# Two experts of up to 64 rows kept on chip in layer 0, slots spread over the partitions, and the modulation product cut along its contraction

## The chip, the cores and the metric

The kernel runs on one core of one Trainium2 chip. The metric is the device time of one execution in microseconds (us), taken as the median over several runs. PE is TensorE, which multiplies matrices, DVE is VectorE, ACT is ScalarE, POOL is GpSimd and SP is SyncE, which here only issues transfers. Weights, gathered rows and results move by DMA between device memory and the chip's buffer.

## The reference, cut to what matters

There are two layers over 512 latent and 256 context tokens of width 1024. Each layer has six modulation vectors, a trunk of four mixers, and a mixture of 32 experts; two experts of one group are chosen for each token.

```python
mod = c_act @ w_ada + b_ada                  # and the same for the context's c
sh1, sc1, g1, sh2, sc2, g2 = jnp.split(mod[:, None, :], N_MOD, axis=-1)
h = modulate(rms_norm(x, norm1_g), sh1, sc1)
...                                          # z = h @ w_in, four mixers, x = x + g1 * merge_groups(...)
h2 = modulate(rms_norm(x, norm2_g), sh2, sc2)
def expert_block(args):
    xb, e = args
    return (jax.nn.silu(xb @ w_gate[e]) * (xb @ w_up[e])) @ w_down[e]
y = y_buf[dest].reshape(n_tok, TOP_K_INNER, d).astype(jnp.float32) * gates[..., None]
x = x + g2 * jnp.sum(y, axis=1)              # layer 0: for 768 tokens, layer 1: for the 512 latent ones
```

All is f32. One expert has 6.29 MB of weights, so the 32 experts of a layer are 201 MB, which are read once in each layer.

## The kernel before, in words

The order on each engine is fixed when the program is built. A layer is a trunk (modulation, the projections `zunits`, the mixers) and then `moe(l)`.

**Modulation.** `w_ada` of a layer (1024 x 6144) is cut into 12 column blocks of 512, `ada(l, j)`, 24 in all; both layers' blocks are computed in trunk 0. The stationary operand is the activated conditioning, two rows (latent and context). A block's four 128-column pieces go to the four column quarters of the array, each through all eight chunks of the contraction: 32 matmuls of 128 columns (L267). Four DVE additions of 2 x 128 (L274) then put each quarter, with the bias, into its own piece of `mrow`. Where the vector is wanted per feature (shift and scale), four small transposes (L280) and a copy into `mcol` (L281) follow; the others go to device memory (`modd`, L293) and are read back, broadcast over the partitions, by `bc` (L301).

**Experts.** Experts are taken by rank of their row count. `CAP` gives the rows that each rank may have, and the number of 32-row steps in it (4 to 1) is its class. The order is ranks 0 and 1, whose weights are loaded ahead of routing; then an interleaving that keeps a running sum of `COST` (a cost by class) near its mean; and last the ranks that stay on chip. PE works through `seq`: gate and up product of place 0, then for each place e gate and up of e (`gu`) and the down product of e-1 (`d`). Weights are issued on SP in the order `lseq`, in half-megabyte slots: 8 for `gu`, 4 for `d`, 34 in layer 0. A load waits until the work that last used its slots is done with them. For each place the gathered rows are transposed (`xTw`), multiplied (L1414), passed through the activation on ACT (L1429) and DVE (L1430), transposed (`hT`) and multiplied by the down weights.

**The end of a layer.** The result of a place below the tail is scaled and scattered by POOL to `yd` (L1762). When the last of these scatters is issued, the layer reads `yd` back, two rows for each token: `yload` (L1804), 1 MB for each group of 128 tokens, six groups (`t`) in layer 0 and four in layer 1, on POOL, into weight slots. The reads stand in `lseq` between weight loads. `accumulate` then weights the two rows (L1491 on ACT, L1494 on DVE), multiplies by the gate `g2` in layer 0 (L1495) and adds to `xres` (L1496). `g2` is read back from `modd` when the last scatter is issued. The tail places (four ranks of up to 32 rows) are not scattered: `tail_rows` (L1482) scales the down result into 32 rows each of one 128-row tile, and a one-hot matrix G, scaled by `tail_scale` (L1366), returns them to their tokens by the matmuls `tailw` (L1791), whose result is added to `xres` (L1792). `finish` takes the sum of squares and its reciprocal root (`rx`, L1814), and the next trunk starts with the normalised and transposed rows (`diag`, L377; `ht`, L334), the `hi` and `lo` parts of its weights (L169, L175) and the products `zunits` (L194 to L196).

```python
for at, ts in ((("gu", NE - 2), range(0, T // 2)), (("d", NE - 3), range(T // 2, T))):
    i = lseq.index(at) + 1
    lseq[i:i] = [("y", t) for t in ts]
```

## Time and profile before

| | |
|---|---|
| median of 3 runs (lowest to highest) | 1895.16 us (1893.27 to 1897.12) |
| time of the profiled execution | 1894.95 us |
| its span, first to last instruction | 1893.2 us |
| trunk 0 and routing / experts of layer 0 | 0 to about 481 / about 481 to 1052 us |
| trunk 1 and routing / experts of layer 1 | to about 1361 / to 1893 us |
| PE busy, DVE busy in the span | 1730.5 us (91%), 744.1 us (39%) |

The stages are read from which lines run when. PE's busy share includes overlapping matmuls and half-speed stretches, so it is no measure of how near a stage is to its limit. The granted clock tells at which speed PE ran; DMA share is the mean busy share of the core's 16 DMA engines.

### The profile page before, as it was taken

What the parts mean: (1) busy time and instruction counts of PE and PEld (TensorE: products, weight loads), DVE (VectorE), ACT (ScalarE), POOL (GpSimd) and SP (SyncE); (2) the same over time, 40 slices, a digit from 0 to 9 for tenths busy, and PEclk for the clock granted to TensorE, in tenths of its full rate; (3) what the DMA queues carried; (4) which work ended last, traced back from release to release, by engine and by line L of the source; (5) the groups of instructions that cost most, each with busy time, mean ns of one, the idle gap of its engine ahead of it and who ended that gap; (6) DMA issues with size and microseconds to landing.
All of it is one profiled execution on the core that took longest, in us unless ns stands there. A gap on an engine that the chain in (4) does not pass through costs nothing.

```text
span 1893.2 us, 32583 instructions
## 1 busy us (share of the span) xinstructions
PE 1730.5 (91%) x12876; PEld 999.2 (53%) x12876; DVE 744.1 (39%) x1627; ACT 467.2 (25%) x842; POOL 221.7 (12%) x253
## 2 busy tenths in 40 slices
PE   6999999998899999999985999999699999989975
PEld 3788788876343433333331788776444433323331
DVE  3666466546211111111116666665523232221135
ACT  4453364322121111111111654732200000000001
POOL 1000100113111111100010001002311110000010
PEclk9999999999799999999986999999799999999987
DMA  8358965453899999999968423428399999999995
GB/s 305 107 188 275 318 227 184 160 211 141 339 414 407 399 398 396 398 401 411 387 229 319 147 87 106 140 76 303 129 366 411 414 410 411 404 401 404 409 414 226
DMA packets 169022, 561.90 MB, mean 297 GB/s; under 512 B 22562, under 2 KB 49250, under 8 KB 139808
## 3 DMA queue, kind: packets, MB, share of 16 engines
q1 hardware_dynamic: 141616, 499.68, 68.9%
q0 software_dynamic: 23072, 54.17, 7.8%
q10 hardware_dynamic: 4176, 5.91, 0.9%
q8 instruction: 104, 1.70, 0.4%
q14 instruction: 54, 0.44, 0.1%
HBM read 544.22 MB, written 35.52 MB: 306 GB/s over the span
## 4 chain that ended last, share of the span: by engine, by line
PE 25%; DMA 18%; DVE 3%; issue 3%; ACT 1%; POOL 0%; SPq 0%; POOLq 0%; ACTq 0%; DVEq 0%
DMA u<-in_w_down 6%; PE gate_up L1414 6%; PE down L1414 3%; DMA u<-in_w_gate 3%; PE zunits L194 2%; PE zunits L195 2%; PE zunits L196 2%; DMA u<-in_w_up 2%; DMA xb<-in_w_down 2%; DMA xb<-in_w_up 1%; DMA xa<-in_w_up 1%; PE transP L838 1%; DMA xc<-in_w_gate 1%; DMA xc<-in_w_up 1%; PE tailw L1791 1%
## 5 line engine op out<-in xcount | busy, mean ns | idle before, releaser
L1414 PE MATMUL gate_up<-u,XT 128*32 128x256 f32 (+4 forms) x1664 | 277.3, 489 | 12.3 <-DMA u<-in_w_up 9.2
L1429 ACT ACTIVATE eh<-gate_up 64x256 f32<-64x256 f32 (+4 forms) x87 | 43.7, 502 | 766.5 <-PE gate_up L1414 745.0
L1414 PE MATMUL gate_up<-xb,XT 128*32 128x256 f32 (+4 forms) x1152 | 215.0, 483 | 12.0 <-DMA xb<-in_w_up 10.6
L1414 PEld LDWEIGHTS gate_up<-u,XT 128*32 128x32 f32 (+4 forms) x1664 | 92.2, 123 | 149.3 <-issue 106.9
L1414 PE MATMUL gate_up<-xa,XT 128*32 128x256 f32 (+4 forms) x680 | 149.8, 488 | 5.3 <-DMA xa<-in_w_up 2.9
L1430 DVE TENSOR_TENSOR eh<-eh,gate_up 64x256 f32<-64x256 f32 (+4 forms) x87 | 50.4, 580 | 256.4 <-ACT eh L1429 253.6
L194 PE MATMUL zunits<-hT,hi 128*128 128x512 f32 (+1 forms) x384 | 140.2, 366 | 0.9 <-ACT cqs L688 0.8
L195 PE MATMUL zunits<-hT,hi 128*128 128x512 f32 (+1 forms) x384 | 136.4, 355 | 0.1
L196 PE MATMUL zunits<-hT,lo 128*128 128x512 f32 (+1 forms) x384 | 135.5, 353 | 0.0
L1414 PE MATMUL gate_up<-xc,XT 128*32 128x256 f32 (+4 forms) x440 | 123.6, 502 | 5.5 <-DMA xc<-in_w_up 4.9
L1414 PEld LDWEIGHTS gate_up<-xb,XT 128*32 128x32 f32 (+4 forms) x1152 | 69.1, 121 | 112.1 <-issue 80.1
L1383 DVE COPY XT<-xTw 128x256 f32<-128x256 f32 (+6 forms) x64 | 44.0, 689 | 209.1 <-PE gate_up L1414 201.8
L1414 PE MATMUL down<-u,ehT 128*32 128x256 f32 (+4 forms) x656 | 109.9, 505 | 5.7 <-DMA u<-in_w_down 5.6
L1762 POOL DMA_INDIRECT yd<-ey,dst x56 | 52.2, 933 | 492.6 <-DVE ey L1474 239.2
L1414 PE MATMUL down<-xb,ehT 128*32 128x256 f32 (+4 forms) x592 | 91.9, 490 | 5.6 <-DMA xb<-in_w_down 5.6
L1474 DVE TENSOR_TENSOR ey<-down,bc 32x256 f32<-32x256 f32 (+7 forms) x112 | 57.7, 515 | 97.1 <-PE down L1414 95.9
L1381 PEld LDWEIGHTS xTw<-cpack,xb 96*128 96x128 f32 (+6 forms) x512 | 61.7, 200 | 51.8 <-issue 22.8
L1381 PE MATMUL xTw<-cpack,xb 96*128 96x96 f32 (+6 forms) x512 | 72.1, 283 | 17.7 <-DVE XT L1383 7.0
L175 DVE TENSOR_TENSOR lo<-u,hi 128x1024 fp32r<-128x1024 f32 (+2 forms) x54 | 65.5, 1217 | 46.0 <-ACT hi L169 45.4
L1472 ACT COPY ey<-down 64x512 f32<-64x512 f32 (+6 forms) x102 | 50.5, 495 | 133.7 <-PE down L1414 132.9
L194 PEld LDWEIGHTS zunits<-hT,hi 128*128 128x128 f32 x384 | 72.8, 190 | 16.0 <-issue 4.4
L1451 DVE COPY ehT<-hT 128x256 f32<-128x256 f32 (+4 forms) x47 | 19.6, 418 | 154.2 <-PE hT L1449 153.7
(397 smaller groups left out, 2898.9 us busy)
## 6 DMA issues: line engine op xcount, KB each, us to landing
u<-in_w_gate SPq DMA_DIRECT2D x112, 512.0 KB
u<-in_w_up SPq DMA_DIRECT2D x106, 512.0 KB
u<-in_w_ada SPq DMA_DIRECT2D x96, 512.0 KB
u<-in_w_down SPq DMA_DIRECT2D x89, 512.0 KB
xb<-in_w_gate SPq DMA_DIRECT2D x37, 1024.0 KB
xb<-in_w_down SPq DMA_DIRECT2D x37, 1024.0 KB
xb<-in_w_up SPq DMA_DIRECT2D x35, 1024.0 KB
xa<-in_w_down SPq DMA_DIRECT2D x26, 1024.0 KB
```

What stands on the lines that cost most here:

```text
L175: self.nc.vector.tensor_sub(o, v, h.bitcast(F32))
L194: mm(out, a[0], b[0], start=start, stop=False)
L195: mm(out, a[0], b[1], start=False, stop=False)
L196: self.lastm = mm(out, a[1], b[0], start=False, stop=stop)
L1381: nc.tensor.transpose(ps[:, k * 128:k * 128 + W], Xv[:, :, k], self.ident[a:a + W, a:a + W])
L1383: nc.vector.tensor_copy(xt, ps.rearrange("p (k n) -> p k n", k=8)[:, :, 0:W])
L1414: self.lastm = self.nc.tensor.matmul(o, x[:, k, a:a + w], m[k // q][:, k % q, c], start=(k == 0), stop=(k == K - 1), tile_position=(0, b))
L1429: self.lasta = nc.scalar.activation(v, ps[0:r, 0:c], AF.Silu)
L1430: self.lastv = nc.vector.tensor_mul(v, v, ps[64:64 + r, 0:c])
L1472: self.nc.scalar.copy(y[a:a + w, c], p[0:w, :])
L1474: self.nc.vector.tensor_mul(y[a:a + w, c], p[0:w, :], g2[b:b + w, c])
L1762: nc.gpsimd.indirect_dma_start(out=self.yd[l][:, :], in_=y, in_offset=None, out_offset=bass.IndirectOffsetOnAxis(ap=R["dst"][0:cap[e], ord ...
```

## The change

The change has these parts.

- Each `CAP` is rounded up to a multiple of 32. The classes of the ranks, and with them the matmul streams, are the same numbers as before: four of class 4, nine of 3, fourteen of 2 and five of 1 in layer 0.
- `TAIL` keeps ranks 25 and 26 (up to 64 rows each) on chip in layer 0, in place of ranks 28 to 31 (up to 32 rows each). `COST` changes slightly. The class of each place in layer 0 was `33142242224224222224232323331111` (with ranks 28 to 31 last) and is `33114141414222232232232322323322`; layer 1 keeps its order.
- In layer 0 all six reads of `yd` now follow the last weights in `lseq`. `g2` is read three scatters earlier. Two groups are accumulated after `gu` of place 31, two after `d` of place 30, and two in the loop over `tailw`. In layer 1 the accumulations stand earlier: one after `gu` of place 30, three after `d` of place 29.
- A table `spread` replaces the plain count in the one-hot comparisons, so that neighbouring rows of an expert lie 4 partitions apart in each block of 32. Which row of an expert lies where is all that differs.
- `ada`: each column quarter takes two of the eight chunks of the contraction and all 512 columns, which makes 8 matmuls of 512 columns in place of 32 of 128; four DVE additions of 2 x 512, each on the sum of the one ahead, add the quarters.

```diff
-CAP = ((96,) * 2 + (128,) * 3 + (104, 96) + (80,) * 4 + (72,) * 2 + (64,) * 3 + (56,) * 5 + (48,) * 5 + (40,) + (32,) * 3
...
+CAP = ((96,) * 2 + (128,) * 4 + (96,) * 7 + (64,) * 14 + (32,) * 5,
+       (96,) * 2 + (96,) * 8 + (64,) * 10 + (32,) * 12)
...
-NTL = 4
+TAIL = ((25, 26), (28, 29, 30, 31))
...
-COST = (24, 19, 13, 8)
+COST = (23, 18, 12.5, 8)
...
-        for k in range(8):
+        for a in range(2):
             for i in range(4):
-                nc.tensor.matmul(ps[32 * i:32 * i + 2, 0:128], self.act[:, k, :],
-                                 w[k // 2][:, k % 2, i * 128:(i + 1) * 128], start=(k == 0), stop=(k == 7),
-                                 tile_position=(0, 32 * i))
+                k = 4 * a + i
+                nc.tensor.matmul(ps[32 * i:32 * i + 2, :], self.act[:, k, :], w[k // 2][:, k % 2, :], start=(a == 0),
+                                 stop=(a == 1), tile_position=(0, 32 * i))
...
         for i in range(4):
-            nc.vector.tensor_add(row[:, i * 128:(i + 1) * 128], ps[32 * i:32 * i + 2, 0:128],
-                                 br[:, i * 128:(i + 1) * 128])
+            nc.vector.tensor_add(row, ps[32 * i:32 * i + 2, :], row if i else br)
...
-        a = slice(32 * j, 32 * j + 32)
-        for n, p in enumerate(py):
-            c = slice(n * 256, (n + 1) * 256)
+        w = py[0].shape[0]
+        a, n = slice(w * j, w * j + w), D // len(py)
+        for i, p in enumerate(py):
+            c = slice(i * n, (i + 1) * n)
             self.lastv = self.nc.vector.tensor_mul(Yr[a, c], p, Gs[a, c])
...
+        self.spread = pp.tile([128, 128], F16, name=f"spread{l}")
+        sv = self.spread.rearrange("p (b c r) -> p b c r", b=4, c=8)
+        for b in range(4):
+            nc.scalar.copy(sv[:, b], self.iota[:, 32 * b:32 * b + 32].rearrange("p (r c) -> p c r", r=4))
...
-        for at, ts in ((("gu", NE - 2), range(0, T // 2)), (("d", NE - 3), range(T // 2, T))):
+        for at, ts in ((("d", NE - 1), range(T)),) if l == 0 else ((("gu", NE - 2), (0, 1)), (("d", NE - 3), (2, 3))):
...
-        na = dict(zip((("gu", NE - 2), ("d", NE - 3), ("gu", NE - 1), ("d", NE - 2)), (1, T // 3, T // 3, 1)))
+        na = {("gu", NE - 1): 2, ("d", NE - 2): 2} if l == 0 else {("gu", NE - 2): 1, ("d", NE - 3): 3}
...
+                    if j == -4 and l == 0:
+                        g2 = [self.bc(self.buf(True), l, 3, m) for m in range(2)]
                     if j == -1:
                         written.append(True)
-                        if l == 0:
-                            g2 = [self.bc(self.buf(True), l, 3, m) for m in range(2)]
...
+        late = list(acc)
         for t in range(T):
+            if t in late:
+                add(t)
```

On POOL, at the end of the experts of layer 0, the order before was this: the scatters of the last three places below the tail (L1762), the reads of `g2` from `modd` (L301) ahead of the last of them, and then the first reads of `yd` (L1804).

```order
L1762 DMA yd_112<-ey_8161,dst_5237 1536x1024
L1762 DMA yd_112<-ey_8291,dst_5237 1536x1024
L301 DMA u_5097<-modd_106 128x1024
L301 DMA u_5098<-modd_106 128x1024
L1762 DMA yd_112<-ey_8402,dst_5237 1536x1024
L1804 DMA u_5099<-yd_112 128x1024
L1804 DMA u_5100<-yd_112 128x1024
```

Now the scatters are L1775, the `g2` reads L300 and the reads of `yd` L1817.

```order
L1775 DMA yd_112<-ey_7633,dst_4666 1536x1024
L300 DMA xb_4_4510<-modd_106 128x1024 x2
L1775 DMA yd_112<-ey_7724,dst_4666 1536x1024
L1775 DMA yd_112<-ey_7838,dst_4666 1536x1024
L1775 DMA yd_112<-ey_7965,dst_4666 1536x1024
L1775 DMA yd_112<-ey_8047,dst_4666 1536x1024
L1817 DMA xc_1_4505<-yd_112 128x2048
L1817 DMA xc_0_4504<-yd_112 128x2048
L1817 DMA u_4517<-yd_112 128x1024
L1817 DMA u_4518<-yd_112 128x1024
```

The reads of `g2` moved from ahead of the last scatter to ahead of the last four, and the reads of `yd` begin with `xc` slots.

On DVE, at the same end, the order before has the first accumulation (L1494 to L1496) ahead of the scaling of the second tail place's result (L1482), and the activations and transposes of later tail places (L1430, L1455) between the accumulations that follow.

```order
L1455 COPY ehT_8544<-hT_8543 64x128 x2
L1430 TENSOR_TENSOR eh_8507<-eh_8507,gate_up_8508 64x256
L1494 SCALAR_TENSOR_TENSOR u_5100<-u_5100,gate_5153,u_5099 128x1024
L1495 TENSOR_TENSOR u_5100<-u_5100,u_5097 128x1024
L1496 TENSOR_TENSOR xres_4380<-xres_4380,u_5100 128x1024
L1482 TENSOR_TENSOR u_5088<-down_8587,xb_2_5084 32x256 x4
L1494 SCALAR_TENSOR_TENSOR u_5090<-u_5090,gate_5153,u_5089 128x1024
L1455 COPY ehT_8657<-hT_8656 64x128
L1495 TENSOR_TENSOR u_5090<-u_5090,u_5097 128x1024
L1455 COPY ehT_8657<-hT_8656 64x128
L1496 TENSOR_TENSOR xres_4380<-xres_4380,u_5090 128x1024
L1494 SCALAR_TENSOR_TENSOR u_5092<-u_5092,gate_5153,u_5091 128x1024
```

Now the last activation of the experts (L1430, of place 31) stands ahead of every accumulation (L1495 to L1497), and one transpose copy of place 31 (L1451) behind the first operation of the first one.

```order
L1430 TENSOR_TENSOR eh_7977<-eh_7977,gate_up_7978 64x512
L1451 COPY ehT_8088<-hT_8087 128x256
L1430 TENSOR_TENSOR eh_8067<-eh_8067,gate_up_8068 64x512
L1495 SCALAR_TENSOR_TENSOR xc_1_4505<-xc_1_4505,gate_4582 128x1024
L1451 COPY ehT_8128<-hT_8127 128x256
L1496 TENSOR_TENSOR xc_1_4505<-xc_1_4505,xb_4_4510 128x1024
L1497 TENSOR_TENSOR xres_3804<-xres_3804,xc_1_4505 128x1024
L1495 SCALAR_TENSOR_TENSOR xc_0_4504<-xc_0_4504,gate_4582 128x1024
L1483 TENSOR_TENSOR u_4512<-down_8102,u_4513 64x512
L1496 TENSOR_TENSOR xc_0_4504<-xc_0_4504,xb_4_4510 128x1024
L1483 TENSOR_TENSOR u_4512<-down_8102,u_4513 64x512
L1497 TENSOR_TENSOR xres_3804<-xres_3804,xc_0_4504 128x1024
```

Behind these rows come three more `tail_rows` operations (L1483; four in all), the rest of the six accumulations and five of the six additions of `tailw` (L1805), and then the first of four `lo` of trunk 1 (L174), with the sixth addition between them, and the first `ht` (L333), for which the first `zunits` waits. Before, the tail places had sixteen `tail_rows` operations of 32 x 256, and all six accumulations stood ahead of the first addition of `tailw`.

On DVE at the start of trunk 0, the first modulation block's additions before (L274, four pieces) and the copy into `mcol` (L281), between the norm's operations (L352, L353):

```order
L274 TENSOR_TENSOR mrow_212<-ada_177,br_210 2x128
L352 RECIPROCAL n1rr_125<-n1s_137 128x1
L274 TENSOR_TENSOR mrow_212<-ada_177,br_210 2x128
L353 TENSOR_SCALAR xn<-xres_75,n1rr_125 128x1024
L274 TENSOR_TENSOR mrow_212<-ada_177,br_210 2x128 x2
L352 RECIPROCAL n1rr_125<-n1s_144 128x1
L353 TENSOR_SCALAR xn<-xres_75,n1rr_125 128x1024
L281 COPY mcol_102<-ada_217 128x8
```

Now each addition reads the sum of the one ahead, and the copy (L280) waits for the fourth:

```order
L274 TENSOR_TENSOR mrow_188<-ada_177,br_186 2x512
L351 RECIPROCAL n1rr_125<-n1s_144 128x1
L274 TENSOR_TENSOR mrow_188<-ada_177,mrow_188 2x512
L352 TENSOR_SCALAR xn<-xres_75,n1rr_125 128x1024
L351 RECIPROCAL n1rr_125<-n1s_151 128x1
L274 TENSOR_TENSOR mrow_188<-ada_177,mrow_188 2x512
L352 TENSOR_SCALAR xn<-xres_75,n1rr_125 128x1024
L351 RECIPROCAL n1rr_125<-n1s_158 128x1
L274 TENSOR_TENSOR mrow_188<-ada_177,mrow_188 2x512
L352 TENSOR_SCALAR xn<-xres_75,n1rr_125 128x1024
L351 RECIPROCAL n1rr_125<-n1s_165 128x1
L280 COPY mcol_102<-ada_193 128x8
```

The four additions lie further apart and are chained, where before any piece could be transposed as soon as it was there.

## Rows read from the trace of the kernel before

**Rows 1.** Windows of 60 us: busy time of PE, PEld, DVE, ACT, POOL; clock; DMA.

```profile
core 0: us, PE busy (x) PEld busy (x) DVE busy (x) ACT busy (x) POOL busy (x), PEclk, DMA share, GB/s
...
600.00:660.00 60.00, 60.00 (x291) 24.75 (x289) 9.14 (x14) 8.76 (x15) 7.88 (x8) 1.00 1.01 401
...
840.00:900.00 60.00, 58.96 (x365) 22.64 (x365) 9.76 (x22) 10.53 (x24) 5.63 (x6) 1.00 1.02 412
...
1440.00:1500.00 60.00, 55.54 (x529) 25.07 (x528) 18.98 (x42) 2.69 (x6) 7.63 (x8) 0.97 1.02 413
...
1800.00:1860.00 60.00, 43.11 (x440) 18.57 (x428) 20.68 (x41) 2.54 (x5) 5.13 (x8) 0.79 1.02 412
```

**Rows 2.** The same columns, longer windows at the end of layer 0's experts.

```profile
940.00:990.00 50.00, 42.86 (x367) 17.95 (x370) 4.94 (x14) 7.72 (x17) 4.00 (x5) 0.90 0.66 243
...
960.00:1000.00 40.00, 30.75 (x351) 14.73 (x344) 5.92 (x16) 6.10 (x14) 7.35 (x12) 0.87 0.65 223
1000.00:1030.00 30.00, 15.03 (x112) 4.01 (x112) 21.73 (x26) 8.76 (x9) 0.53 (x1) 0.53 1.02 412
```

**Rows 3.** The chain that ended last, 941 to 1056 us: start, duration, what.

```profile
941.48 20.14 issue
...
961.87 0.94 POOL yd L1762
...
962.94 7.46 DMA u<-modd
...
992.08 10.40 DMA xc<-in_w_up
...
1002.50 23.68 DMA u<-in_w_down
...
1026.22 1.13 PE down L1414 x8
...
1036.36 10.39 PE tailw L1791 x20
...
1046.77 1.22 DVE xres L1792
...
1052.39 2.42 DVE lo L175 x2
1054.81 0.12 DVE diag L377
1054.93 0.74 DVE ht L334
```

**Rows 4.** DVE by lines, 985 to 1054 us: busy, mean ns, idle before.

```profile
L1792 DVE TENSOR_TENSOR xres<-xres,tailw 128x1024 f32<-128x1024 f32 x6 | 7.3, 1220 | 4.3 <-PE tailw L1791 4.1
...
L1494 DVE SCALAR_TENSOR_TENSOR u<-u,gate,u 128x1024 f32<-128x1024 f32 x3 | 3.9, 1284 | 8.2 <-DMA u<-yd 7.5 <-issue 0.7
L1496 DVE TENSOR_TENSOR xres<-xres,u 128x1024 f32<-128x1024 f32 x3 | 3.7, 1226 | 0.1
L1495 DVE TENSOR_TENSOR u<-u,u 128x1024 f32<-128x1024 f32 x3 | 3.7, 1219 | 0.1
L175 DVE TENSOR_TENSOR lo<-u,hi 128x1024 fp32r<-128x1024 f32 x3 | 3.6, 1219 | 0.5 <-ACT hi L169 0.5
...
L377 DVE TENSOR_SCALAR diag<-cpack,rx 128x128 f32<-128x128 f32 x4 | 1.1, 283 | 0.4 <-PE norm L379 0.4
L1814 DVE RECIPROCAL rx<-fsd 128x1 f32<-128x1 f32 x6 | 0.8, 154 | 0.0
```

**Rows 5.** DVE line L1474, all its shapes: ns min/median/max.

```profile
L1474 DVE TENSOR_TENSOR ey<-down,bc x112: 411/425/693, 1403.2 to 1822.7; 32x256 f32<-32x256 f32 x32, 64x512 f32<-64x512 f32 x20, 24x256 f32<-24x256 f32 x20, 8x256 f32<-8x256 f32 x16
```

**Rows 6.** POOL line L1762, the scatters: issue to landing.

```profile
L1762 POOL DMA_INDIRECT yd<-ey,dst x56: 878/929/1037, 523.6 to 1823.4; - x56
...
DMA to landing us min/median/max: 3.8/7.1/11.5
```

**Rows 7.** DVE lines L274 and L292, and who waited for L274.

```profile
L274 DVE TENSOR_TENSOR mrow<-ada,br x96: 269/284/293, 19.1 to 338.3; 2x128 f32<-2x128 f32 x96
...
  PEld ada L280: 4.8, 10
  PE ada L280: 1.9, 3
...
L292 DVE SCALAR_TENSOR_TENSOR mrow<-mrow,ng x4: 669/670/673, 153.7 to 312.5; 2x512 f32<-2x512 f32 x4
```

**Rows 8.** Windows as in rows 1, of trunk 0.

```profile
130.00:140.00 10.00, 10.00 (x138) 9.04 (x137) 8.23 (x22) 5.00 (x9) 0.51 (x1) 1.00 0.95 322
...
130.00:210.00 80.00, 79.01 (x1125) 65.08 (x1123) 53.63 (x156) 29.58 (x61) 7.12 (x15) 1.00 0.86 283
120.00:340.00 220.00, 217.69 (x2616) 180.46 (x2615) 138.19 (x360) 100.22 (x180) 21.82 (x36) 1.00 0.76 250
```

**Rows 9.** PE by lines: modulation, 120 to 340 us, and quarter-wide products, 865 to 880 us.

```profile
L267 PE MATMUL ada<-u,cact 128*2 128x128 f32 x1216 | 37.7, 272 | 1.5 <-DMA u<-in_w_ada 1.3
...
L1414 PE MATMUL gate_up<-u,XT 128*32 128x256 f32 x28 | 1.9, 382 | 0.0
```

**Rows 10.** The chain that ended last, at the end of layer 1.

```profile
1842.98 19.75 DMA xa<-in_w_up
...
1873.01 1.28 DVE xres L1499
1874.29 0.01 issue
1874.31 0.42 DVE xb L1482
1874.72 0.01 issue
1874.74 0.43 DVE xb L1482
...
1875.21 5.41 PE tailw L1791 x8
```

More of the change, by code (lines that the diff above doesn't have):

```diff
@@ L27 @@
 GT = (0, 1, 1, 2)
-CAP = ((96,) * 2 + (128,) * 3 + (104, 96) + (80,) * 4 + (72,) * 2 + (64,) * 3 + (56,) * 5 + (48,) * 5 + (40,) + (32,) * 3
-       + (32,) * 2,
-       (96,) * 2 + (96, 96, 88, 80) + (72,) * 4 + (56,) * 2 + (48,) * 2 + (40,) * 6 + (32,) * 4 + (24,) * 4 + (32,) * 4)
+CAP = ((96,) * 2 + (128,) * 4 + (96,) * 7 + (64,) * 14 + (32,) * 5,
+       (96,) * 2 + (96,) * 8 + (64,) * 10 + (32,) * 12)
 OCAP = (128, 96)
@@ L1234, in route @@
         for a in range(0, NB, 4):
-            nc.vector.tensor_tensor(sl[:, a:a + 4, :], self.iota.unsqueeze(1).to_broadcast([128, 4, 128]),
+            nc.vector.tensor_tensor(sl[:, a:a + 4, :], self.spread.unsqueeze(1).to_broadcast([128, 4, 128]),
                                     bcst(place[:, a:a + 4], 128), op=OP.is_equal)
@@ L1315, in tail_table @@
         NB = 2 * T
+        NTL = len(TAIL[l])
+        TR = 128 // NTL
         start, cnt = R["col"][:, 0:1], R["col"][:, 1:2]
@@ L1331, in tail_table @@
         ta = pp.tile([128, NB, NTL], F32, name=f"ta{l}")
-        for i in range(NTL):
-            e = NE - NTL + i
+        for i, e in enumerate(TAIL[l]):
             nc.vector.tensor_scalar(ta[:, :, i], posf, SL[:, e:e + 1], None, op0=OP.subtract)
@@ L1340, in tail_table @@
         self.G, self.Yr = self.buf(True)[:, 0:T * 128], self.buf(True)
-        sh = [128, 2, NTL, 32]
+        sh = [128, 2, NTL, TR]
         for t in range(T):
@@ L1345, in tail_table @@
             nc.vector.tensor_tensor(eq.rearrange("p (k i e) -> p k i e", k=2, i=NTL),
-                                    self.iota[:, 0:32].unsqueeze(1).unsqueeze(1).to_broadcast(sh),
+                                    self.spread[:, 0:TR].unsqueeze(1).unsqueeze(1).to_broadcast(sh),
                                     ta[:, 2 * t:2 * t + 2, :].unsqueeze(3).to_broadcast(sh), op=OP.is_equal)
@@ L1621, in moe @@
         order = [0, 1]
-        rest = list(range(2, NE - NTL))
+        NTL = len(TAIL[l])
+        rest = [r for r in range(2, NE) if r not in TAIL[l]]
         cost = lambda r: len(COST) - -(-CAP[l][r] // QW)
@@ L1630, in moe @@
             ahead += COST[i] - mean
-        order += range(NE - NTL, NE)
+        order += TAIL[l]
         cap = [CAP[l][r] for r in order]
@@ L1745, in moe, with add @@
         acc = iter(range(T))
-        na = dict(zip((("gu", NE - 2), ("d", NE - 3), ("gu", NE - 1), ("d", NE - 2)), (1, T // 3, T // 3, 1)))
+        def add(t):
+            self.accumulate(l, t, Y[t], R["gate"], g2)
+            for x in held.pop(("y", t)):
+                x[1] = False
+        na = {("gu", NE - 1): 2, ("d", NE - 2): 2} if l == 0 else {("gu", NE - 2): 1, ("d", NE - 3): 3}
         for i, (m, e) in enumerate(seq):
@@ L1778, in moe @@
             for _ in range(na.get((m, e), 0)):
-                t = next(acc)
-                self.accumulate(l, t, Y[t], R["gate"], g2)
-                for x in held.pop(("y", t)):
-                    x[1] = False
+                add(next(acc))
         for _ in tt:
```

## The prediction

> **What bounds the kernel now.** First the windows along the span, for where PE or the DMA engines set the pace. In the middle of layer 0's experts both do: PE is busy for 60 of 60 us at full clock and the DMA share is 1.00 to 1.02 at 401 to 412 GB/s; in layer 1's experts DMA stays at 1.02 while PE falls to 43.11 of 60 [rows 1]. So nothing that saves PE or DVE time there is worth anything by itself. An expert's 6.29 MB take 15.3 us at 412 GB/s, whatever its class.
>
> Then the end of layer 0's experts, where this breaks. In 940 to 990 us the DMA share is 0.66: the engines lie idle for 0.34 x 50 = 17.0 us. In 1000 to 1030 they are full again, but PE has work for half of the time, at clock 0.53 [rows 2]. The chain tells why [rows 3]. POOL issues the reads of `g2` and the scatter behind them only at about 962, after 20.14 us that the chain gives to no wait; `g2` takes 7.46 us more, and only then `tail_scale` and the tail's products go on. The reads of `yd` need the last scatter, and in the load order two weight loads of the tail stand behind them. So the last weights come at 1002.50 + 23.68 = 1026.2, behind 6.3 MB of `yd` (6.3 / 412 = 15.3 us). Then eight down matmuls, the tail's rows, `tailw` from 1036.4 and the additions follow, and trunk 1's first `ht` starts at 1054.9.
>
> Last the end of layer 1: the last weights come at 1842.98 + 19.75 = 1862.7 and later, and two DVE operations of an accumulation and the last rows end at 1875.2, where `tailw` starts [rows 10].
>
> **The end of layer 0.** Three things are to be priced: when the last weights can be there, when PE is through, and when DVE is.
>
> Weights: no read of `yd` stands ahead of a weight load any more, and nothing of the experts waits for `g2` at the end. Both the idle 17.0 us and the 15.3 us of `yd` leave the way of the last weights: 1026.2 - 17.0 - 15.3 = 994.
>
> PE: the classes are the same multiset, so the work to the last down product is the same. From 960 to 1030 PE did 30.75 us at clock 0.87 and 15.03 at 0.53 [rows 2], or 26.8 + 8.0 = 34.8 us at full clock, so that it could be through at 960 + 34.8 = 995, if it waits no more ahead of 960 than it did. Weights and PE come to the same point; with the last quarter of a down product behind the last weights I take 997. The new order alternates class 1 and class 4 at places 2 to 10. A buffer of 34 slots is 2.8 experts, and a cheap and a dear one together need the 31 us that two experts' weights take, by the planner's own costs of 8 and 23, so I charge it nothing; the bound is one class-1 place lost, 8 us, which the range holds.
>
> DVE: place 29's scatter is issued two down products and one gate-and-up product ahead of PE's end. I put place 29's down product at about 981; scaling takes one operation on each half, the issue 0.93 and the landing 3.8 to 7.1 us [rows 6], so 987 to 990. The first 1 MB of `yd` shares the DMA with the last weights and can be there at 993 to 997, its scaling on ACT at 997 at the latest of these. From there the order on DVE up to the first `ht` is fixed: six accumulations of 1.28 + 1.22 + 1.23 = 3.73, or 22.4; four `tail_rows` of at most 0.69 [rows 5], 2.8; six additions of 1.22, 7.3; four `lo` of 1.22, 4.9; five `diag` and six `rx`, 2.3 [rows 4]. Together 39.7 us. One wait is sure: between the last `tail_rows` and the first addition stands a single operation of 1.22, and `tailw` of one group (4 of the 20 records that took 10.39 us, 2.1 us) [rows 3], at half clock after PE has idled, is longer; I allow 3 us for it and for what comes late. So `ht` at 997 + 39.7 + 3 = 1039.7 instead of 1054.9: **-15**. Bounds: a start at 993 with no wait gives -22; a start at 1003 (a scatter at the longest landing, 11.5, or PE late by a place) with 6 us of waits gives -6. `g2`'s earlier reads (1 MB) only move in a stream that is full, 2.6 us of DMA either way.
>
> The one-hot comparisons read another table of as many elements, and four copies on ACT, which is idle for 50 of 60 us there, build it: nothing. Rounded capacities send some more rows in a scatter or transpose; the matmul streams don't change: nothing. `spread` could shorten a scatter's landing if rows reach the DMA engines more evenly; with a mean share of 1.00 there is nothing to even out in mid-stretch, and the bound is the 7.1 - 3.8 = 3.3 us between the median and the quickest landing [rows 6], once, at the last scatter.
>
> **Layer 1.** Same order, same loads, DMA at 1.02: no gain in the middle. At its end the last 1.28 of an accumulation leaves the chain [rows 10], but the last down product sets the rows after it: -0.5, between 0 and -1.3.
>
> **Modulation.** DVE: an addition of 2 x 128 takes 0.284, an operation of 2 x 512 takes 0.670 [rows 7]; four make 2.68 instead of 1.14, so 24 blocks add 24 x 1.54 = 37 us to DVE, all in trunk 0. There PE is at 79.0 of 80 us and 217.7 of 220, DVE at 53.6 of 80 in the densest stretch, with 8.23 of 10 at its peak [rows 8]. Twelve blocks fall into these 80 us: 53.6 + 18.5 = 72.1. It still fits, but with less slack for the `lo` and `ht` that PE wants. At the start the copy into `mcol` waits for the whole chain, and nothing covers it: +1.5. For the rest the bounds are 0 and 37; the nearest row is what PE waited for `mrow` before its transposes, 4.8 + 1.9 us in all [rows 7], and I take +3. **+4.5** together, 0 to 12 as its likely span.
>
> By the Trainium skill (TensorEngine Tiling (Array Packing), section PSUM Bottleneck), cutting the array into tiles speeds the matmuls but not the evacuation of their results, which may become the bottleneck; this change makes that evacuation 2.4 times as long. Were it the bottleneck, the 37 us would show and the kernel would be slower; the row of 53.6 busy of 80 says that it is not yet.
>
> PE: a block's 64 records (two for each f32 matmul) took 37.7 / 19 = 1.98 us; now there are 16, four times as wide. That quarters run side by side at greater width is seen in 28 records of 256 columns that take 1.9 us while each lasts 382 ns [rows 9]: 68 ns each, so 136 at 512 columns, or 2.2 us for a block, with the pipeline's filling counted in. Four times the 31 ns of now gives 1.98. So 0 to +0.2 for each, 0 to +5 in all; the filling weighs on 28 records, so I take 0.
>
> **The sum.** -15 - 0.5 + 4.5 = -11. The profiled execution took 1894.95 us (0.2 below the median), so **1884**.
>
> **Rivals.** *The chain of additions overloads trunk 0* (slower). For it: the peak of 8.23 of 10, and the next block's first addition writes the same single `mrow` that the last block's transfer still reads. Against it: 26 us of slack in the densest 80. It decides from 19.5 us of its 37 on, where the gain of 15.5 and the bound of 0.2% are used up; with 22 to 24 of them it is 1894.95 - 15.5 + 23 = 1902. Chance 0.12.
>
> *DVE takes the place of DMA at the end of layer 0* (no change). All six accumulations now lie behind the last weights, where before DVE was busy for 21.7 of the 30 us of the last transfers [rows 2], and a transpose copy of place 31 stands behind the first of them: if `yd` comes late, PE's last product waits too. With the first group ready only at 1008, `ht` is at 1008 + 39.7 + 3 = 1050.7, a gain of 4, and the modulation takes it: 1894 to 1896. For it: the first read shares the DMA with the last weights, and a scatter's landing reaches 11.5 us [rows 6]. Against it: PE and the weights both point to 995. Chance 0.12.
>
> *The new order starves PE* (smaller gain). If alternating classes let the buffer run full or dry once, 8 us of the 15 go: 1892 at most, mostly 1887 to 1890. Chance 0.12.
>
> *All is hidden* (larger gain). DVE starts at 993, no wait, the modulation's adds are covered: -22 - 1.3 + 0, with the quicker landing down to -26: 1869 to 1874. Chance 0.12.
>
> *The forecast*, 1876 to 1888, has 0.52. A change under 0.2% (3.8 us) could not be told from none with this kernel. Counting half of the starving case's upper end as none: faster 0.74, same 0.13, slower 0.13. The range, 1868 to 1899, leaves out the slow rival and a little of the last one.
>
> **What would show it.** Right: a DMA share near 1.00 from 540 to about 1005 without the gap of 0.66; no wait of `tail_scale` for `g2`; the last weights of place 31 landing near 994 and `ht` near 1040 plus what trunk 0 lost; DVE busy almost without a gap from 997 on; trunk 0 ending 3 to 6 us later, with L274 at 0.67 each. Wrong: the first accumulation after 1005; PE waiting for weights between 500 and 940; trunk 0 later by over 15 us, or not at all; matmuls of modulation that take over 2.2 us for a block. What would upset the sum most is a `yd` read that waits for a slot or a scatter, since 40 us of DVE work now hang on the first.

## The result, and the profile after

The changed kernel takes 1920.59 us (median of 4 runs, 1913.17 to 1923.24) against 1896.14 for the kernel before beside it: a ratio of 1.0121, with a 95% interval of 1.0099 to 1.0142. (Ratios, here and below, are formed from the runs in the faster of the chip's states and need not equal the quotient of the medians.) It is slower by 19 to 27 us, where 11 us less was forecast. Its profiled execution is the longest of the four, 1923.24 us with a span of 1921.4, 28.3 us above that of before; of differences between two profiles a few us may be the execution and not the kernel. (The section on the change gives the classes of layer 0 before with two digits wrong, at places 17 and 19, counted from 0: they were `33142242224224222323232323331111`. No number was worked out from these digits.)

Stage by stage, by the same events in both traces. The first activation of layer 0's experts, before and after:

```profile
498.25 0.59 ACT L1429 ACTIVATE eh<-gate_up 64x512 f32<-64x512 f32 x1 [21.74 <-PE gate_up L1414]
```

```profile
527.06 0.59 ACT L1429 ACTIVATE eh<-gate_up 64x512 f32<-64x512 f32 x1 [21.57 <-DMA u<-in_w_gate]
```

It ends at 498.8 us before and at 527.7 after: 28.8 us are lost in trunk 0. From there to the first `ht` of trunk 1 it is 556.1 before and 555.4 after, where 15 less were forecast. From there to layer 1's first activation, and from that to the end, it is the same within 1 us.

Trunk 0 first. Windows of 60 us of the changed kernel, with the columns of rows 1:

```profile
0.00:60.00 60.00, 36.76 (x192) 20.30 (x192) 29.99 (x63) 27.50 (x49) 7.22 (x10) 1.00 0.79 269
60.00:120.00 60.00, 59.01 (x346) 49.14 (x350) 33.90 (x62) 26.88 (x49) 4.18 (x6) 1.00 0.32 97
120.00:180.00 60.00, 57.21 (x452) 36.59 (x444) 49.21 (x110) 23.91 (x47) 3.15 (x6) 1.00 0.73 237
180.00:240.00 60.00, 45.36 (x302) 31.66 (x298) 33.03 (x74) 12.98 (x28) 3.31 (x9) 0.80 0.60 205
```

The same windows of the kernel before:

```profile
0.00:60.00 60.00, 42.14 (x398) 28.73 (x399) 29.10 (x68) 29.21 (x52) 7.18 (x10) 1.00 0.79 278
...
120.00:180.00 60.00, 59.13 (x878) 50.18 (x877) 43.95 (x122) 23.82 (x48) 5.13 (x12) 1.00 0.84 281
180.00:240.00 60.00, 58.56 (x627) 47.49 (x624) 28.63 (x78) 23.88 (x44) 9.30 (x13) 1.00 0.92 305
```

PE idles 5.4 us more at the start and 13.2 more in 180 to 240, though DVE is busy for only 33 of these 60 us. In the last window PE was also granted a lower clock, 0.80 for 1.00, which makes its 45.4 us of work there worth about 9 us less (an estimate, 45.4 x 0.20). The clock fell after PE had begun to idle:

```profile
180.00:190.00 10.00, 7.98 (x54) 4.75 (x50) 5.68 (x11) 2.25 (x4) 0.50 (x1) 1.00 0.54 179
190.00:200.00 10.00, 5.02 (x17) 3.01 (x15) 7.99 (x18) 2.16 (x4) 1.19 (x5) 0.54 0.74 259
```

In the second of these PE was granted the lower of its two levels, 1.2 of 2.4 GHz, for nearly all of the time. Up to the first activation PE idles 65.7 us instead of 42.1, and it is busy for 5.2 us longer, at a mean clock of 0.95 instead of 0.97. The chained additions themselves, line L274 of the changed kernel (ns min/median/max), and who waited for them:

```profile
L274 DVE TENSOR_TENSOR mrow<-ada,mrow x72: 681/685/694, 20.7 to 368.8; 2x512 f32<-2x512 f32 x72
...
  PE ada L279: 16.0, 4
  PEld ada L279: 15.7, 3
```

An addition takes 0.685 us (0.67 forecast). PE's transposes waited 16.0 us at four places for the chain's last link, where they had waited 1.9 [rows 7]. These 14.1 us are the largest part of the 23.6 that PE idles more; 3.1 more stand ahead of the same transposes with `nmx` named as what ended them, and 6.8 ahead of products of the attention and the projections that wait for `P` or `yM`. DVE in time order around one such place (start, duration, line; brackets: idle before):

```profile
196.28 0.68 DVE L274 TENSOR_TENSOR mrow<-ada,br 2x512 f32<-2x512 f32 x1 [1.28 <-DMA modd<-mrow]
196.89 0.14 DVE L824 RECIPROCAL prc<-psm 128x1 f32<-128x1 f32 x1
196.96 0.18 DVE L816 TENSOR_SCALAR nmx<-mx,rq 128x1 f32<-128x1 f32 x1
197.17 0.68 DVE L274 TENSOR_TENSOR mrow<-ada,mrow 2x512 f32<-2x512 f32 x1
197.79 0.60 DVE L826 TENSOR_SCALAR P<-P,prc 128x768 f32<-128x768 f32 x1
198.41 0.68 DVE L274 TENSOR_TENSOR mrow<-ada,mrow 2x512 f32<-2x512 f32 x1
199.13 0.42 DVE L811 TENSOR_REDUCE mx<-mla_itemw 128x1 f32<-128x256 f32 x1
```

The links alternate with the softmax of the attention (maximum `mx`, its scaled negative `nmx`, reciprocal `prc`, scaling of `P`), and each delays the other.

Then the end of layer 0's experts, windows of the changed kernel:

```profile
990.00:1020.00 30.00, 29.48 (x175) 10.05 (x175) 3.22 (x7) 4.66 (x10) 1.85 (x2) 0.89 0.95 355
1020.00:1040.00 20.00, 20.00 (x114) 6.21 (x112) 1.68 (x4) 4.50 (x9) 3.31 (x6) 1.00 0.14 40
1040.00:1050.00 10.00, 7.54 (x34) 2.32 (x30) 6.64 (x8) 5.12 (x6) 2.93 (x6) 1.00 0.98 381
1050.00:1080.00 30.00, 19.55 (x57) 10.37 (x58) 28.68 (x35) 15.23 (x26) 2.13 (x4) 0.83 0.72 252
```

The gap of 0.66 in the DMA share [rows 2] is gone, and the weights are all there by about 1020 us. But now PE works on for more than 20 us with the DMA engines idle, and only then does DVE begin. The chain that ended last says on what:

```profile
1033.52 0.91 DMA yd<-ey,dst
1034.43 3.15 issue
...
1037.60 5.18 DMA xc<-yd
...
1042.80 1.16 ACT xc L1492
...
1043.98 1.30 DVE xc L1495
...
1056.12 5.35 PE tailw L1804 x6
...
1078.49 1.14 DVE lo L174
```

The last scatter, the first read of `yd`, and from 1043.98 the list on DVE. It reaches the first `ht` 39.0 us later, by DVE in time order:

```profile
1083.01 1.42 DVE L333 SCALAR_TENSOR_TENSOR ht<-norm,a,hT 128x512 f32<-128x512 f32 x2 [0.61 <-ACT hT L332]
```

### The profile page after: what moved, and what is told of

Same layout as the page of the kernel before. It is cut to its first block, busy times and chain, and to the rows that moved or that the text cites. A ratio compares the mean times of both kernels' runs of the same rounds, so it can differ in the third digit from the quotient of the medians.

```text
span 1921.4 us, 30267 instructions
## 1 busy us (share of the span) xinstructions
PE 1745.2 (91%) x11724; PEld 986.7 (51%) x11724; DVE 776.4 (40%) x1611; ACT 471.0 (25%) x862; POOL 222.1 (12%) x255
## 5 line engine op out<-in xcount | busy, mean ns | idle before, releaser
L1414 PE MATMUL gate_up<-u,XT 128*32 128x256 f32 (+1 forms) x1608 | 275.2, 489 | 10.5 <-DMA u<-in_w_up 8.1
L1414 PE MATMUL gate_up<-xb,XT 128*32 128x256 f32 (+1 forms) x1160 | 211.0, 481 | 6.1 <-DMA xb<-in_w_up 5.0
L1414 PE MATMUL gate_up<-xa,XT 128*32 128x256 f32 (+1 forms) x816 | 172.6, 480 | 7.7 <-DMA xa<-in_w_up 4.8
L1414 PEld LDWEIGHTS gate_up<-u,XT 128*32 128x32 f32 (+1 forms) x1608 | 93.4, 125 | 138.6 <-issue 97.0
L1430 DVE TENSOR_TENSOR eh<-eh,gate_up 64x512 f32<-64x512 f32 (+1 forms) x87 | 50.5, 580 | 276.3 <-ACT eh L1429 274.5
L1414 PEld LDWEIGHTS gate_up<-xb,XT 128*32 128x32 f32 (+1 forms) x1160 | 70.5, 123 | 104.2 <-issue 78.9
L1414 PE MATMUL down<-u,ehT 128*32 128x256 f32 (+1 forms) x736 | 117.9, 479 | 0.9 <-DMA u<-in_w_down 0.6
L1775 POOL DMA_INDIRECT yd<-ey,dst x58 | 53.4, 921 | 516.3 <-ACT ey L1472 271.6
L1414 PE MATMUL gate_up<-xc,XT 128*64 128x512 f32 (+1 forms) x352 | 110.5, 520 | 2.1 <-DMA xc<-in_w_up 2.1
L1414 PE MATMUL down<-xb,ehT 128*32 128x256 f32 (+1 forms) x584 | 96.7, 508 | 6.6 <-DMA xb<-in_w_down 4.7
L1474 DVE TENSOR_TENSOR ey<-down,bc 32x256 f32<-32x256 f32 (+1 forms) x112 | 57.7, 516 | 96.2 <-PE down L1414 95.0
L1381 PE MATMUL xTw<-cpack,xb 64*128 64x64 f32 (+3 forms) x512 | 75.2, 283 | 22.5 <-DVE XT L1383 10.0
L1381 PEld LDWEIGHTS xTw<-cpack,xb 64*128 64x128 f32 (+3 forms) x512 | 63.2, 200 | 59.5 <-issue 25.6
L174 DVE TENSOR_TENSOR lo<-u,hi 128x1024 fp32r<-128x1024 f32 (+2 forms) x54 | 65.4, 1217 | 43.5 <-ACT hi L168 40.8
```

Source lines behind the costliest of these rows:

```text
L174: self.nc.vector.tensor_sub(o, v, h.bitcast(F32))
L1381: nc.tensor.transpose(ps[:, k * 128:k * 128 + W], Xv[:, :, k], self.ident[a:a + W, a:a + W])
L1414: self.lastm = self.nc.tensor.matmul(o, x[:, k, a:a + w], m[k // q][:, k % q, c], start=(k == 0), stop=(k == K - 1), tile_position=(0, b))
L1430: self.lastv = nc.vector.tensor_mul(v, v, ps[64:64 + r, 0:c])
L1474: self.nc.vector.tensor_mul(y[a:a + w, c], p[0:w, :], g2[b:b + w, c])
L1775: nc.gpsimd.indirect_dma_start(out=self.yd[l][:, :], in_=y, in_offset=None, out_offset=bass.IndirectOffsetOnAxis(ap=R["dst"][0:cap[e], ord ...
```

## The experiments

All ratios are to the kernel before, run beside them on the same chip.

**e1: the change without its modulation.** `ada` as before, all else changed.

```diff
-                nc.tensor.matmul(ps[32 * i:32 * i + 2, :], self.act[:, k, :], w[k // 2][:, k % 2, :], start=(a == 0),
-                                 stop=(a == 1), tile_position=(0, 32 * i))
+                nc.tensor.matmul(ps[32 * i:32 * i + 2, 0:128], self.act[:, k, :],
+                                 w[k // 2][:, k % 2, i * 128:(i + 1) * 128], start=(k == 0), stop=(k == 7),
+                                 tile_position=(0, 32 * i))
...
-            nc.vector.tensor_add(row, ps[32 * i:32 * i + 2, :], row if i else br)
+            nc.vector.tensor_add(row[:, i * 128:(i + 1) * 128], ps[32 * i:32 * i + 2, 0:128],
+                                 br[:, i * 128:(i + 1) * 128])
```

> The changed kernel with the modulation product as before: 32 matmuls of 128 columns, four independent additions of 2 x 128. Theory A (the chain of four additions of 2 x 512 and the block of transposes that waits for it on PE cost the 28.8 us by which the first expert's activation comes later): that activation is back at about 499 us, and the time is about 27 below the changed kernel's, 1891 to 1897. Theory B (the loss in trunk 0 has other causes: the table for the slots, or another order of the other work): it stays within 6 us of the changed kernel's, 1913 to 1922.

Measured: 1889.92, ratio 0.9965 (0.9950 to 0.9980); the first activation at 500.7 us. Theory A holds: the modulation is the whole loss, and the rest of the change gains 4 to 9 us.

**e2: the kernel before with the new modulation alone** (the same diff the other way round).

> The kernel before with only the modulation product of the change. Theory A: 1895 + 27 = about 1922, the same loss in trunk 0 as in the changed kernel (first activation of the experts at about 527 us). Theory B: below 1903.

Measured: 1924.37, ratio 1.0135 (1.0107 to 1.0164), first activation at 525.1 us. Theory A again, from the other side.

**e5 and e6: which blocks.** The new product in only some of the 12 blocks of each layer, on the kernel before: the diff is that of e5, and e6 has `j >= 4`.

```diff
+        new = j < 4
...
+            if new:
+                nc.vector.tensor_add(row, ps[32 * i:32 * i + 2, :], row if i else br)
+            else:
+                nc.vector.tensor_add(row[:, i * 128:(i + 1) * 128], ps[32 * i:32 * i + 2, 0:128],
+                                     br[:, i * 128:(i + 1) * 128])
```

> The kernel before with the new modulation product only in the 8 blocks of shift and scale, which are transposed on PE (16 blocks stay as they were). Theory A1 (PE stalls because its transposes, and what is queued behind them, wait for the last link of the chain; the trace of the changed kernel puts 31.7 us of PE's waits in front of L279): most of the 29 us are lost, 1915 to 1924. Theory A2 (what counts is the work added to DVE, 37 us over 24 blocks, wherever it stands): a third of it, about 1904 to 1906.

> The complement: the new product only in the 16 blocks that go to device memory and have no transposes on PE; 24.6 us are added to DVE. Theory A1: 1895 to 1900. Theory A2: two thirds of 29 us, 1912 to 1916.

Measured: e5 1903.55, ratio 1.0037 (1.0017 to 1.0057), 3 to 11 us; e6 1914.09, ratio 1.0088 (1.0066 to 1.0111), 13 to 21 us. I had come to hold A1, since the wait in front of the transposes is the largest that the view of waits shows. It fell as the whole account: the blocks without transposes lose about two thirds, their share of the added DVE work, with 4.6 us of PE's waits for `mrow` in e6. (With the whole change PE's wait at the transposes is still its largest.)

**e9: DVE work alone.** The kernel before with its own product, and additions that nobody uses.

```diff
+        for i in range(3):
+            nc.vector.tensor_add(ps[32 * i:32 * i + 2, 128:512], br[:, 0:384], br[:, 128:512])
```

> The kernel before with its own modulation product, and for each block three more DVE additions of 2 x 384 that nothing uses, written behind the product in its own PSUM tile: about 1.6 us more of DVE work for each of the 24 blocks, near the 1.54 of the change, with no link of a chain that another engine waits for. Theory A2 (e5 and e6 lost 7 to 9 and 17 to 19 us for a third and two thirds of the work: DVE time in trunk 0 costs about 0.7 of itself, wherever it stands): 1915 to 1925. Theory A3 (only additions that someone waits for cost, or the wide product itself): below 1902.

Measured: 1916.72, ratio 1.0111 (1.0084 to 1.0138), 16 to 26 us. The additions took 0.559 us each, 72 of them, 40 us in all. So DVE work in trunk 0 costs time though nobody waits for its result, with the product on PE as it was (the additions hold its PSUM tile and the tile of the bias a little longer, which may be a part; PE's waits that end with these additions are 1.1 and 0.5 us). Where it goes is seen in PE's waits up to 480 us:

```profile
PE ada L282 <- DVE mrow L274: 9.1, 4, 5.1
...
PE mla_itemw L194 <- ACT P L825: 3.6, 3, 3.2
PE transP L840 <- DVE P L829: 3.0, 1, 3.0
PE transP L840 <- DVE yM L917: 2.2, 3, 0.9
```

The first had been 1.9 us before [rows 7], and the other three were not there. So additions without a reader stand on DVE's queue ahead of others that PE does wait for: 7.2 us more at the transposes of the modulation, 8.8 in the attention (its scores `mla_itemw` and the transposes of `P`). The granted clock falls here too, to 0.91 in 180 to 240 us, where it was 1.00.

ACT, which takes the exponentials of the softmax behind DVE's `nmx`, does not show the loss. Its row in 120 to 240 us before (last columns: idle before, and its releaser):

```profile
L823 ACT ACTIVATE P<-mla_itemw,nmx,rq 128x768 f32<-128x768 f32 (+1 forms) x22 | 18.4, 837 | 16.2 <-DVE nmx L817 14.1 <-DVE a L286 1.2 <-DVE prc L825 0.4
```

The same of e9:

```profile
L825 ACT ACTIVATE P<-mla_itemw,nmx,rq 128x768 f32<-128x768 f32 (+1 forms) x23 | 19.4, 845 | 18.4 <-DVE nmx L819 15.6 <-PE transP L840 2.6 <-DVE prc L827 0.2
```

The wait for `nmx` is 15.6 us in e9 and 14.1 before; in e6 it is 26.5, and in e10, which loses next to nothing, 22.7 (below).

**e10: half as much.** Two chains of two additions of 2 x 256.

```diff
+                k, c = 4 * (i % 2) + a, 256 * (i // 2)
+                nc.tensor.matmul(ps[32 * i:32 * i + 2, 0:256], self.act[:, k, :], w[k // 2][:, k % 2, c:c + 256],
+                                 start=(a == 0), stop=(a == 3), tile_position=(0, 32 * i))
...
+            o = row[:, 256 * (i // 2):256 * (i // 2) + 256]
```

> The kernel before with a middle form of the product: each column quarter takes half of the contraction and half of the columns (16 matmuls of 256 columns), and two chains of two additions of 2 x 256 follow, about 4 x 0.42 = 1.68 us of DVE for each block instead of 1.14 before and 2.74 in the change. Theory A2: 24 x 0.54 x 0.7 = 9 us slower, 1902 to 1907. If the length of the chain decides instead (two links for four), about half of the loss, 1908 to 1912.

Measured: 1899.75, ratio 1.0014 (0.9994 to 1.0033). Both expectations miss. ACT's row here:

```profile
L823 ACT ACTIVATE P<-mla_itemw,nmx,rq 128x768 f32<-128x768 f32 (+1 forms) x22 | 18.4, 838 | 23.3 <-DVE nmx L817 22.7 <-PE ada L268 0.4
```

For the same 22 exponentials ACT waits 8.6 us longer for `nmx` than before, and yet the kernel is hardly slower; PE's wait for `mrow` is 6.9 us. The cost seems less than in proportion: 13 us of added DVE work cost -1 to 6, 40 cost 16 to 26, but at the lowest rate of e9, 0.40, 13 us would cost 5, which lies within the interval. What decides how much is absorbed is not settled; e5, with about as much added work in fewer and longer operations, lost 3 to 11, and had PE wait 13.8 us before its transposes.

**e3: the order of before for layer 0's experts,** on e1.

```diff
-TAIL = ((25, 26), (28, 29, 30, 31))
+TAIL = ((28, 29, 30, 31), (28, 29, 30, 31))
...
-COST = (23, 18, 12.5, 8)
+COST = (24, 19, 13, 8)
```

> As e1, and ranks 28 to 31 kept on chip in layer 0 with the costs of before, so that the order of experts in layer 0 is that of before; the reads of yd behind the last weights, the early read of g2 and the places of the accumulations stay changed. Theory C (the new order puts class-1 places where DMA sets the pace, and leaves class 2 and 3 behind the last weights, which costs about 20 us of PE at the end of layer 0; the moved reads of yd and g2 gain what was forecast): 12 to 20 us below e1, about 1877 to 1883. Theory D (the order is worth nothing, and the moved reads gain little because DVE's list of 39 us hangs on the first of them): within 5 us of e1.

**e4: the class-1 places moved behind the others,** on e1.

```diff
+        if l == 0:
+            order = [r for r in order if cost(r) < 3] + [r for r in order if cost(r) == 3]
         order += TAIL[l]
```

> As e1, with ranks 25 and 26 kept on chip, but the five class-1 places moved from places 2 to 9 to places 25 to 29, right ahead of the two that stay on chip; the other classes move up. Theory C: PE no longer waits for weights in the early places and has cheap work behind the last weights: the last activation of layer 0's experts comes 10 to 16 us earlier after the first than in e1, and the time is 8 to 16 us below e1. Theory D: within 4 us of e1.

Measured: e3 1890.65, ratio 0.9959 (0.9932 to 0.9986); e4 1888.09, 0.9964 (0.9942 to 0.9986). In time that is e1 again, as theory D has it. In the trace theory C is seen too: the last activation of layer 0's experts ends 512.7 us behind the first in e1, 504.4 in e4 and 499.4 in e3. When PE has done its gate-and-up products does hang on the order, by 8 to 13 us. It gains little because something else is late next. In e3 the two reads of the first group are issued at 996.87 and 997.43, and ACT and DVE wait for them:

```profile
1005.03 1.15 ACT L1492 ACTIVATE xb<-xb,gate 128x1024 f32<-128x1024 f32 x1 [2.77 <-DMA xb<-yd]
```

```profile
1007.65 1.28 DVE L1495 SCALAR_TENSOR_TENSOR xc<-xc,gate,xb 128x1024 f32<-128x1024 f32 x1 [4.94 <-DMA xc<-yd]
```

A read of the second group takes longer still, by the chain:

```profile
998.50 12.94 DMA xc<-yd
```

PE's longest wait there:

```profile
PE down L1414 <- DVE ehT L1455: 15.7, 1, 15.7
```

With PE early, the first reads of `yd` are issued while the last weights still stream. They take 8.2 and 10.2 us in e3, for half a megabyte each, and 9.2 in e4 (1000.20 to 1009.40) for a whole one, instead of the 5.18 of the changed kernel. The second transpose copy of place 31 (1019.55 on DVE) stands behind two accumulations that wait for such reads, and PE's last down product behind the copy: it ends 520.5 us behind the first activation in e3, hardly earlier than the 521.7 of e1. That is the mechanism of the prediction's second rival. The first `ht` still comes 6.7 us (e3) and 3.6 us (e4) earlier than in e1, counted from the first activation; e3's trunk 0 was 2.1 us longer in the profiled execution, which takes part of it.

**e7: `g2` alone,** on the kernel before.

```diff
+                    if j == -4 and l == 0:
+                        g2 = [self.bc(self.buf(True), l, 3, m) for m in range(2)]
                     if j == -1:
                         written.append(True)
-                        if l == 0:
-                            g2 = [self.bc(self.buf(True), l, 3, m) for m in range(2)]
```

> The kernel before with the read of g2 three scatters earlier, and nothing else. If the 7.46 us wait for g2 and the scatter behind it set the start of the tail, 5 to 8 us faster, 1887 to 1890. If the last weights, which wait for slots under the reads of yd, set the end anyway, within 2 us of before.

Measured: 1890.93, ratio 0.9981 (0.9966 to 0.9996): 1 to 6 us, 3.7 of them in the stretch to the first `ht` (552.4 instead of 556.1). Between the two expectations: PE's wait for the read of `g2` (6.5 us before) is gone, and about half of it reaches the first `ht`; what takes the rest is not traced. It cannot be told from the gain of e1, so this small part may be most of what the change gained.

**e8: no spread,** on e1: the plain count in both comparisons.

```diff
-self.spread.unsqueeze(1).to_broadcast([128, 4, 128])
+self.iota.unsqueeze(1).to_broadcast([128, 4, 128])
```

> As e1 (the changed kernel with the old modulation product), with the plain count instead of the spread table, so that the rows of an expert lie on neighbouring partitions. Theory: a DMA share of 1.0 leaves nothing to even out, within 2 us of e1, 1888 to 1892. Rival: the spread rows shorten gathers and scatters, and this is 4 us or more slower than e1.

Measured: 1891.57, ratio 0.9979 (0.9963 to 0.9995), against 0.9965 for e1. As the theory has it, no difference that these runs can tell.

**e11 and e12: the product by `g2` on POOL,** on e4 and on e3.

```diff
-                nc.vector.tensor_mul(y1, y1, g2[t // 4])
+                nc.gpsimd.tensor_mul(y1, y1, g2[t // 4])
```

> As e4 (old modulation product, class-1 places late), with the product by g2 in the accumulations of layer 0 moved from DVE to POOL. Theory E (the end of layer 0 is the arrival of the first group of yd and then DVE's list of 39 us): six times 1.22 us leave DVE's list, POOL does them in 2.4 us each beside it, and the first ht comes 4 to 7 us earlier than in e4: 1881 to 1885. Rival: a POOL product of 2.4 us between two DVE operations of the same group is on the list all the same, and the time is within 2 us of e4 or slower.

> As e3 (old modulation product, ranks 28 to 31 on chip in layer 0, order of before), with the product by g2 on POOL. Theory E: the wait of the last down product for a transpose copy that stands behind accumulations on DVE (15.7 us in e3) shrinks and the list is shorter: 4 to 8 us below e3, 1883 to 1887. Rival as for e11: within 2 us of e3.

Measured: e11 1891.27, ratio 0.9980 (0.9960 to 1.0000), no gain over e4; e12 1882.79, ratio 0.9929 (0.9903 to 0.9955), the quickest version here, 9 to 18 us below the kernel before. That e12 is quicker than e3 is not shown by the times, since the intervals overlap; in the trace the first `ht` comes at 544.3 us behind the first activation instead of 548.6 in e3. Its chain shows what is left:

```profile
988.52 12.45 DMA xc<-yd
...
1002.96 2.38 POOL xc L1496
...
1006.50 1.29 DVE u L1495
```

In e11 the read of the first group takes 9.2 us (998.95 to 1008.13), one behind it 12.46. Products on POOL and operations on DVE then run at the same time, and some of both get longer. DVE in time order in e11:

```profile
1013.88 1.92 DVE L1495 SCALAR_TENSOR_TENSOR u<-u,gate,u 128x1024 f32<-128x1024 f32 x1 [1.54 <-ACT u L1492]
1015.72 1.21 DVE L1497 TENSOR_TENSOR xres<-xres,xc 128x1024 f32<-128x1024 f32 x1
1016.86 3.37 DVE L1495 SCALAR_TENSOR_TENSOR xc<-xc,gate 128x1024 f32<-128x1024 f32 x1
1020.14 1.21 DVE L1497 TENSOR_TENSOR xres<-xres,u 128x1024 f32<-128x1024 f32 x1
```

POOL in time order there:

```profile
1012.34 2.36 POOL L1496 TENSOR_TENSOR xc<-xc,xb 128x1024 f32<-128x1024 f32 x1
1015.88 3.26 POOL L1496 TENSOR_TENSOR u<-u,xb 128x1024 f32<-128x1024 f32 x1 [1.17 <-DVE u L1495]
1020.30 3.25 POOL L1496 TENSOR_TENSOR xc<-xc,xb 128x1024 f32<-128x1024 f32 x1 [1.16 <-DVE xc L1495]
```

In each of the four overlaps it is the operation that started second that gets longer, by about what was left of the first: 1.92 and 3.37 us for 1.28 on DVE, 3.26 and 3.25 for 2.36 on POOL. By the Trainium skill (Advanced Engine Details and Errata, section GPSIMD Details), the Pool engine shares a read and a write interface with DVE and conflicts with DVE instructions of two inputs in the chip's buffer; this trace agrees, with 1.92 and 3.37 for 1.28. In e12's chain the product ended at 1005.34, ahead of the DVE operation at 1006.50, which took 1.29. The first `ht` of e11 came 1.8 us later than in e4. Theory E is seen in the trace of one of two orders.

## Why the prediction was wrong

**What bounds the kernel.** Right for the middle of the experts and for the stall of `g2` (e7), but the windows of trunk 0 were read wrongly, see below.

**Modulation, +4.5.** This is the step that failed most: it measured +29 in the profiled execution, and 20 to 31 by the ratio of e2. The additions were sized rightly (0.685 for 0.670), although the densest 80 us hold 40 of them, ten blocks and not twelve. PE's part was right too: a block's 16 records of 512 columns ran in 1.90 us (at 39.1 us, where nothing interrupts them), and PE gained or lost nothing there. What failed is the sentence that 53.6 + 18.5 = 72.1 of 80 us "still fits". A busy share of two thirds [rows 8] was taken for slack of a third. In this stretch DVE is one station of a loop (PE's scores, DVE's maximum, ACT's exponential, DVE's scaling, PE's transposes), and what is added to its queue delays whatever PE waits for next, with or without a reader of its own (e9). So the 3 us taken from the nearest row, 6.7 us of PE's waits for `mrow`, became 23.6 us that PE idles more, 17.2 of them ahead of the modulation's transposes; the +1.5 at the start became 5.4. The sum also had no term for the clock, which fell to 0.80 in 180 to 240 us once PE idled. How much of an addition is absorbed, and where the rest comes out, stays open: e6 loses 13 to 21 us with the transposed blocks as before, e5 3 to 11 with them alone, and e10 almost nothing. The rival named the right place and a price of 23, with a chance of 0.12. Its condition, the single `mrow`, is seen as 7.3 us of DVE's waits for the last block's transfer (1.3 before); no run gives `mrow` a second buffer.

By the Trainium skill (TensorEngine Tiling (Array Packing), section PSUM Bottleneck) the evacuation may become the bottleneck when tiles speed up the matmuls. The trace agrees that the evacuation came to cost time, though the matmuls got no faster (1.90 us for 1.98) and nothing was saturated: DVE was busy for 33 of 60 us where PE lost most.

**The end of layer 0, -15.** It measured -0.7 from the first activation to the first `ht`. Of its three parts, the weights were right: forecast at 994, they were there by about 1020, which is 991 after the later start is taken off. DVE's list was right: 39.7 forecast, 39.0 measured. The failing part is PE "through at 960 + 34.8 = 995, if it waits no more ahead of 960 than it did". Its last down product ended at 1049.4, or 1020.6 without the later start. Windows from 960 us on the clock of the kernel before to the last down product, of the changed kernel:

```profile
988.80:1049.43 60.63, 58.22 (x322) 18.96 (x318) 10.98 (x18) 13.80 (x23) 8.09 (x13) 0.94 0.69 256
```

Of e3 and of e4:

```profile
964.00:1023.33 59.33, 43.02 (x497) 20.22 (x488) 22.93 (x39) 15.39 (x25) 8.20 (x14) 0.80 0.96 367
```

```profile
959.20:1018.81 59.61, 48.21 (x280) 17.48 (x280) 13.02 (x20) 11.86 (x22) 7.92 (x13) 0.83 1.02 415
```

By the prediction's own reckoning, busy time times clock, PE had 54.7 us of work left there instead of 34.8, and e1 with the modulation of before as much (58.13 us at 0.94 from 961.9 to 1022.4); with the order of before (e3) it had 34.4, with the class-1 places last (e4) 40.0. So it is the order: the same multiset of classes doesn't leave the same work for the end. With the cheap places early PE falls behind in the middle, where the weights set the pace. In 540 to 960 us it idled 11.1 us instead of 3.3, of which 2.5 were waits for weights and 5.5 waits for gathered rows and the copies of their transposes; the rest of the 20 us I have not traced. The rival "the new order starves PE" had the right place, priced at 8. With PE late, the scatter of place 29 was issued at 1033.52 and landed at 1037.6 (1008.8 without the later start) instead of 987 to 990, and the first accumulation began at 1044.0 (1015.2) instead of 997. All of the gain went there.

But e3 and e4 also show that an earlier PE would not have brought the -15: the first reads of `yd` then share the DMA with the last weights for 8 to 10 us. I had priced the arrival of the first group at 993 to 997; it was there 504.8 us (e3) and 511.3 us (e4) behind the first activation, which is about 1004 and 1010 on the clock of the kernel before. A row of the kernel before had the price; its reads of `yd` (L1804, both layers) took:

```profile
DMA to landing us min/median/max: 8.0/15.7/24.0
```

**Layer 1, -0.5**: from its first activation to the end 513.6 before and 512.9 after. Right. **Spread, 0**: right (e8).

## What to carry to other kernels

An engine's idle share is slack only if nobody waits at the end of its idle stretches: ahead of adding work to a half-idle engine, read what the other engines of its loop wait for, and count that PE's idling can cost clock as well (0.80 here). Work that is kept behind the last transfer should be the cheapest, and the work that hides under transfers the dearest (e3 and e4 end their last activation 13 and 8 us earlier than e1); that two orders do the same work says nothing of when it ends. When a list is moved behind one event, everything ahead of that event is on the path, so price its first arrival with what else is in flight then.

## What was not expected of the hardware

When a DVE operation of two tensors and a POOL product overlap, the one that starts second waits out about the rest of the first: in e11 the DVE operation took 1.92 and 3.37 us instead of 1.28, and the POOL product 3.26 and 3.25 instead of 2.36, while the one ahead kept its time (1.21 on DVE, 2.36 on POOL). And operations on two partitions only, 40 us of them spread over 350 us of a half-busy DVE, cost 16 to 26 us (e9).
